# An encoder kernel on one core: the first sum of a layer's seven-product units, put behind the last combination of the right sides

## The chip, the cores and the metric

The kernel runs on one core of a Trainium2 chip. The metric is the device time in microseconds (us) of one execution; smaller is better. The engines of the core work side by side, each through its own queue of instructions in order: TensorE (PE: matmuls, and PEld: its weight loads), VectorE (DVE), ScalarE (ACT), GpSimd (POOL) and SyncE (SP). In this kernel SP issues nearly all loads, and POOL issues the accumulating loads. Matmuls read SBUF and write PSUM, which has eight banks; the kernel uses them as four pairs, named acc, sc, o and aux.

## The reference

Two layers of a bidirectional encoder over a sequence of 512 rows of width 1024, in float32. Each layer has a mixing part (retention heads and differential attention heads behind one input projection, and an output projection) and then a gated feed-forward part, which is the one that matters here:

```
h = rms_norm(x, ffn_norm_g[l])
x = x + (silu(h @ w_gate[l]) * (h @ w_up[l])) @ w_down[l]
```

`w_gate` and `w_up` are 1024 x 2816, `w_down` is 2816 x 1024. The normalisation scales each row of x by one over its root mean square and each column by `ffn_norm_g`.

## The kernel before

The activations are kept transposed: `x` is eight tiles of 128 features by 512 rows. Every product is done to full precision by splitting both sides into a high part (a cast on ACT) and a low part (the remainder, a subtraction on DVE) and adding three matmuls: high by high, high by low, low by high (`mm3`, lines 204 to 208). So each weight that arrives by DMA first costs one ACT cast (line 194) and one DVE subtraction (line 198), and each activation likewise (lines 223 and 224, in `split`).

The feed-forward part takes the 22 blocks of 128 columns of the gate and up projections in four groups, `FFN = [(0, 4), (4, 12), (12, 18), (18, 22)]`. After each group comes the down projection of that group, `for m in range(KT)` (lines 818 to 847): for each of eight column blocks m of the output, the weights of the group are loaded (two column blocks at a time in the first group), split (lines 194 and 198), multiplied into a PSUM bank, and added to `x[m]` by a DVE addition, `residual`, line 634. The banks come in turn from acc, sc and o, two of each, so six column blocks can be under way; blocks 6 and 7 need banks that the residuals of blocks 0 and 1 have emptied.

The first group is done plainly (`gate_up`, lines 681 to 695). The other three use units of seven products in place of eight for a pair of 2 x 2 blocks (`seven`, lines 751 to 797). For that the right sides, that is the halves of the normalised `x`, must be added and subtracted with one another once in each layer. This is `combine(i)` (lines 715 to 736), called four times: `combine(0)` to `combine(2)` while the plain group runs, after its blocks 1, 2 and 3 (line 805), and `combine(3)` inside the first down projection, after its column block 1 (line 845). Each makes, on DVE, the scaled halves `b1`, `b2` (line 719), four sums `ta` and `tb` (lines 721 to 724), and the splits of all of them (lines 712, 728 and, through `split`, 224). The split of `tb` (line 730) comes last.

The left sides are combined too, for each unit. A unit has two rows of weights of 128 x 1024 in `in_wgu`. It loads one block twice into a tile by a broadcast load (line 756, SP), loads another block (line 757, SP) and the second row (line 758, SP), and has two more blocks added to the first tile on their way in, by an accumulating load (line 759, POOL):

```
nc.gpsimd.dma_start(sums, src[:, 0::3], accum_op=ALU.add)
i = nc.vector.tensor_tensor(a[:, T:], a[:, :T], s31[:, T:], op=ALU.add)
```

Line 760 is the sum that this case is about: it reads what the accumulating load has left, and line 763 adds its result to the second row's first half (`s4`). Then come the unit's casts and splits (lines 740 and 741, in `split_in`, and `split` for `s4`) and its 84 matmuls of 128 x 256 (line 775). The tile of a (and of the sum) is called s or raw in the profile, in turn from unit to unit; in the first unit of a layer the sum is s<-s,raw.

The order of the work on each engine is not written in the kernel: the Tile framework puts it out by its own model of times and priorities, from the order of the code and the dependencies. The kernel can add an ordering edge, `tc.add_manual_dep(later, earlier, order, ...)`, which says that one instruction is put behind another; between instructions of one engine it costs no semaphore. Before the change the sum of each unit has such an edge to the last split of the unit before, kept in `last_split[0]` (lines 741, 761 and 762). The first unit of a layer has none, since `last_split[0]` is `None` there.

Of the kernel before, what the change touches and what calls it, by code (L numbers as in the profile page):

```python
# [11 lines left out]
ALU = mybir.AluOpType  # L12
# [42 lines left out]
def encoder_kernel(ctx: ExitStack, tc: tile.TileContext, xT, wfirst, wsingle, wvv, wout, wgu, wdn, prm, lam, cst, outT):  # L55
    nc = tc.nc
# [14 lines left out]
    def big(s, dt=F32, tag="w", bufs=NW):  # L71
        return tpool.tile([P, T], dt, tag=tag, name=nm(s), bufs=bufs)
# [19 lines left out]
    def f32(ap):  # L92
        return ap.bitcast(F32)
# [42 lines left out]
    def column_sums(ps, w, src):  # L136

        hi, lo = split(src, "w", NW)
        nc.tensor.matmul(ps, w, hi, start=True, stop=False)
        sums[0] = nc.tensor.matmul(ps, w, lo, start=False, stop=True).ins.name  # L140
# [40 lines left out]
    def pair():  # L181

        t = tpool.tile([P, 2, T], F32R, tag="h", name=nm("h"), bufs=8)
        return t[:, 0], t[:, 1]
# [25 lines left out]
    def cut(pair, *idx):  # L210
        return tuple(t[idx] for t in pair)
# [9 lines left out]
    def split(src, tag, bufs):  # L221
        hi, lo = pair() if tag == "h" else [big(n, F32R, tag, bufs) for n in ("hi", "lo")]
        nc.scalar.copy(hi, src)
        nc.vector.tensor_tensor(lo, src, f32(hi), op=ALU.subtract)
        return hi, lo

    def rsqrt(out, src, scale):

        func(out, src, AF.Ln, bias=eps_sb, scale=scale)
        func(out, out, AF.Exp, scale=-0.5)  # L230
# [79 lines left out]
    def layer(l, n1, h, x_src, first_raw):  # L310
# [76 lines left out]
        def diff_head(hd, qs, ks, v):  # L387
# [42 lines left out]
            rsqrt(sq, ss, 1.0 / P)  # L430
            nc.vector.scalar_tensor_tensor(sq, o, gd[:, l : l + 1], sq, op0=ALU.mult, op1=ALU.mult)
            mix[4 + hd] = split(sq, "mix", NMIX)
            yield

        def ret_pair(pr):
# [80 lines left out]
            nc.vector.scalar_tensor_tensor(sq, o, prm_sb[:, PRM_RG + l : PRM_RG + l + 1], sq, op0=ALU.mult, op1=ALU.mult)  # L516
            nc.vector.tensor_tensor(sq, sq, gates[pr], op=ALU.mult)
            mix[pr] = split(sq, "mix", NMIX)
            yield "norm"

# [182 lines left out]


        H1, H2 = slice(0, C), slice(C, T)
        comb = []

        def part256(src):
            hi = tpool.tile([P, 256], F32R, tag="dv", name=nm("bh"), bufs=16)
            lo = tpool.tile([P, 256], F32R, tag="dv", name=nm("bl"), bufs=16)  # L710
            nc.scalar.copy(hi, src)
            nc.vector.tensor_tensor(lo, src, f32(hi), op=ALU.subtract)
            return hi, lo

        def combine(i):

            b1, b2 = big("b"), big("b")
            for t, kt in ((b1, i), (b2, i + 4)):
                nc.vector.scalar_tensor_tensor(t, x[kt], prm_sb[:, PRM_FG + 8 * l + kt : PRM_FG + 8 * l + kt + 1], rstd2, op0=ALU.mult, op1=ALU.mult)
            ta, tb = big("ta"), big("tb")  # L720
            nc.vector.tensor_tensor(ta[:, H1], b1[:, H1], b1[:, H2], op=ALU.subtract)
            nc.vector.scalar_tensor_tensor(ta[:, H2], ta[:, H1], -1.0, b2[:, H2], op0=ALU.mult, op1=ALU.subtract)
            nc.vector.tensor_tensor(tb[:, H1], b2[:, H2], b1[:, H2], op=ALU.subtract)
            nc.vector.scalar_tensor_tensor(tb[:, H2], ta[:, H2], -1.0, b2[:, H1], op0=ALU.mult, op1=ALU.subtract)
            b11, b21 = part256(b1[:, H1]), part256(b2[:, H1])
            b22 = big("b22", F32R, *[("w", NW), ("qk", NQK), ("mix", NMIX), ("mix", NMIX)][i])
            nc.scalar.copy(b22[:, H1], b2[:, H2])
            nc.vector.tensor_tensor(b22[:, H2], b2[:, H2], f32(b22[:, H1]), op=ALU.subtract)
            ta = split(ta, "mix", NMIX)
            tb = split(tb, *(("mix", NMIX) if i else ("qk", NQK)))  # L730
            comb.append(
                dict(
                    b11=b11, b21=b21, b22=(b22[:, H1], b22[:, H2]),
                    t1=cut(ta, slice(None), H1), t2=cut(ta, slice(None), H2), t3=cut(tb, slice(None), H1), t4=cut(tb, slice(None), H2),
                )
            )
# [9 lines left out]
            fours[0] += 1  # L746
            return new_chunk(1024)[0] if fours[0] % 2 else tpool.tile([P, 1024], F32, tag="ah", name=nm("s"), bufs=NAH)

        fours, last_split = [0], [None]

        def seven(ff, act, tag, bufs):

# [46 lines left out]
        for a0, a1 in FFN:  # L799
            act, last = [], a1 == FT  # L800
            if a1 <= PLAIN:
                for ff in range(a0, a1):
                    act.append(gate_up(ff, *(("mix", NMIX) if ff < 2 else ("rn", 4))))
                    if ff:
                        combine(ff - 1)
            else:
                units = []
                for ff in range(a0, a1):
                    tag = ("h", 8) if not last else ("mix", NMIX) if ff < a0 + 2 else ("rn", 4)
                    units.append(seven(ff, act, *tag))  # L810
                next(units[0])
                for i, unit in enumerate(units):
                    next(unit)
                    if i + 1 < len(units):
                        next(units[i + 1])
                    next(unit, None)
            n = (a1 - a0) * P
            for m in range(KT):

                both = 2 * n <= 1024  # L820
                if not both or m % 2 == 0:
                    new = new_chunk(n * (1 + both), 1)
                    for i in range(1 + both):
                        nc.sync.dma_start(new[0][:, i * n : (i + 1) * n], wdn[l, m + i][:, a0 * P : a1 * P])
                    ww = split_chunk(*new)
                w = cut(ww, slice(None), slice(m % 2 * n, (m % 2 + 1) * n)) if both else ww
                if last and l + 1 == DEPTH and m == KT - 1:

                    for t, queue in ((H1, nc.sync), (H2, nc.scalar)):
                        ps = any_bank()  # L830
                        for i, a in enumerate(act):
                            mm3(ps[:, :C], cut(w, slice(None), slice(i * P, (i + 1) * P)), cut(a, slice(None), t), i == 0, i == a1 - a0 - 1)
                        nc.vector.tensor_tensor(x[m][:, t], x[m][:, t], ps[:, :C], op=ALU.add)
                        queue.dma_start(outT[m][:, t], x[m][:, t])
                    continue
                ps = any_bank()
                for i, a in enumerate(act):
                    mm3(ps, cut(w, slice(None), slice(i * P, (i + 1) * P)), a, i == 0, i == a1 - a0 - 1)
                if last and l + 1 < DEPTH:
                    residual(m, x[m], ps, n3, h3, PRM_AG + 8 * (l + 1))  # L840
                    nc.sync.dma_start(xscr[m], x[m])
                else:
                    residual(m, x[m], ps, None, None, None)
                    if a1 <= PLAIN and m == 1:
                        combine(PLAIN - 1)
                    if last:
                        nc.sync.dma_start(outT[m], x[m])
# [10 lines left out]
    for l in range(DEPTH):  # L858
        if l:
            raws = [load_chunk(wfirst[l, c]) for c in range(4)]  # L860
        n, h = layer(l, n, h, xT if l == 0 else xscr, raws)
# [89 lines left out]
```

## Time and profile before

| what | us |
|---|---|
| median of 3 runs | 1265.05 |
| lowest and highest run | 1262.17 and 1267.66 |
| the profiled execution | 1264.07 |
| its span, from first to last instruction | 1262.3 |
| TensorE busy | 1247.4 |
| DVE busy | 915.8 |
| ACT busy | 674.1 |

The first down projection of layer 0 begins at about 324 us of the span, the first seven-product unit at about 350 us; in layer 1 these are about 948 and 976 us. A row of a view in order of time has the start, the duration, the engine, the line of the kernel, the operation, the tile written and the tiles read (buffer numbers left out), the shapes, the count, and in brackets the idle time of the engine ahead of it with the party that ended it. The duration of a matmul is longer than the distance to the next one's start, because matmuls overlap; so distances between starts count for TensorE. The granted clock is the share of TensorE's full clock.

### The profile page before, as it was taken

To read this page: it belongs to the slowest core of one execution; us is meant where nothing else is said; L and a number is where in the kernel's file an instruction comes from. 1 tells how busy PE (TensorE), PEld (TensorE's weight loads), DVE (VectorE), ACT (ScalarE), POOL (GpSimd) and SP (SyncE) were. 2 spreads that over 40 slices of the span, in tenths; PEclk is the share of its full clock that TensorE was granted. 3 is DMA by queue.
4 is the path that set the end of the run, shared out by engine and by line. 5 is a ranking of instruction groups with operands and counts; after the bars stand their busy time and mean duration, and the time that the engine had idled before them with its cause. 6 is when DMAs were issued, how large, how long until landed. Compare 5 with 4: busy or idle time off the path is not lost.

```text
span 1262.3 us, 19138 instructions
## 1 busy us (share of the span) xinstructions
PE 1247.4 (99%) x7516; PEld 1100.3 (87%) x7516; DVE 915.8 (73%) x1514; ACT 674.1 (53%) x1106; POOL 61.4 (5%) x78
## 2 busy tenths in 40 slices
PE   9999999999899999999999999999999999999998
PEld 7878988778799989989888889987887999899897
DVE  6899768867877546747568997697778775576574
ACT  6778746555445425525448785565553553254251
POOL 1000000000011001000000000000000110000000
PEclk9999999999999999999999999999999999999999
DMA  7222223243277537646342122142333774476452
GB/s 264 84 68 67 68 67 125 68 116 101 71 176 174 166 102 166 163 114 151 110 156 84 51 84 67 51 150 77 99 101 84 174 182 129 119 180 152 122 140 84
DMA packets 58842, 148.48 MB, mean 118 GB/s; under 512 B 5632, under 2 KB 5888, under 8 KB 58624
## 3 DMA queue, kind: packets, MB, share of 16 engines
q1 hardware_dynamic: 48528, 127.95, 32.8%
q0 software_dynamic: 9792, 18.88, 9.4%
q8 instruction: 59, 0.97, 0.3%
q10 hardware_dynamic: 432, 0.44, 0.1%
q14 instruction: 31, 0.25, 0.1%
HBM read 143.05 MB, written 4.19 MB: 117 GB/s over the span
## 4 chain that ended last, share of the span: by engine, by line
PE 94%; DVE 3%; DMA 1%; ACT 1%; issue 0%; ACTq 0%
PE acc L775 16%; PE acc L205 11%; PE acc L207 11%; PE acc L206 11%; PE o L775 8%; PE o L205 4%; PE o L207 4%; PE sc L775 4%; PE o L206 4%; PE sc L207 4%; PE sc L205 4%; PE sc L206 3%; PE sc L400 2%; PE o L501 2%; PE sc L485 1%; DMA raw<-in_wgu 1%
## 5 line engine op out<-in xcount | busy, mean ns | idle before, releaser
L194 ACT CAST hi<-raw 128x1024 fp32r<-128x1024 f32 (+2 forms) x139 | 138.2, 1002 | 185.8 <-issue 49.2
L198 DVE TENSOR_TENSOR lo<-raw,hi 128x1024 fp32r<-128x1024 f32 (+2 forms) x140 | 162.1, 1162 | 58.8 <-ACT hi L194 58.4
L205 PE MATMUL acc<-h,hi 128*128 128x512 f32 x406 | 160.1, 396 | 0.6 <-ACT hi L194 0.6
L206 PE MATMUL acc<-h,hi 128*128 128x512 f32 x406 | 159.4, 393 | 0.0
L207 PE MATMUL acc<-h,lo 128*128 128x512 f32 x406 | 159.4, 393 | 0.0
L775 PE MATMUL acc<-hi,hi 128*128 128x256 f32 x432 | 123.2, 285 | 0.0
L775 PE MATMUL acc<-hi,lo 128*128 128x256 f32 x432 | 122.3, 283 | 0.0
L775 PE MATMUL acc<-lo,hi 128*128 128x256 f32 x432 | 122.3, 283 | 0.0
L740 ACT CAST hi<-raw 128x1024 fp32r<-128x1024 f32 x54 | 56.7, 1050 | 72.3 <-PE acc L775 42.2
L741 DVE TENSOR_TENSOR lo<-raw,hi 128x1024 fp32r<-128x1024 f32 x54 | 66.2, 1225 | 38.1 <-ACT hi L740 38.1
L740 ACT CAST hi<-s 128x1024 fp32r<-128x1024 f32 x54 | 56.6, 1048 | 67.3 <-issue 25.6
L205 PEld LDWEIGHTS acc<-h,hi 128*128 128x128 f32 x406 | 76.5, 189 | 17.6 <-ACT hi L194 1.9
L207 PEld LDWEIGHTS acc<-h,lo 128*128 128x128 f32 x406 | 76.6, 189 | 16.1 <-DVE lo L198 0.2
L206 PEld LDWEIGHTS acc<-h,hi 128*128 128x128 f32 x406 | 76.6, 189 | 15.2
L741 DVE TENSOR_TENSOR lo<-s,hi 128x1024 fp32r<-128x1024 f32 x54 | 66.2, 1226 | 25.4 <-ACT hi L740 25.4
L775 PEld LDWEIGHTS acc<-lo,hi 128*128 128x128 f32 x432 | 82.9, 192 | 0.2
L775 PEld LDWEIGHTS acc<-hi,hi 128*128 128x128 f32 x432 | 82.7, 192 | 0.2
L775 PEld LDWEIGHTS acc<-hi,lo 128*128 128x128 f32 x432 | 82.8, 192 | 0.0
L106 ACT ACTIVATE g<-g 128x512 f32<-128x512 f32 x44 | 27.8, 632 | 52.7 <-DVE g L793 47.8
L106 ACT ACTIVATE sc<-sc,mx 128x512 f32<-128x512 f32 x64 | 46.0, 720 | 18.4 <-DVE mx L404 17.9
L205 PE MATMUL sc<-h,hi 128*128 128x512 f32 x142 | 55.5, 394 | 0.0
L206 PE MATMUL sc<-h,hi 128*128 128x512 f32 x142 | 55.4, 390 | 0.0
(235 smaller groups left out, 3500.4 us busy)
## 6 DMA issues: line engine op xcount, KB each, us to landing
raw<-in_wgu SPq DMA_DIRECT2D x52, 512.0 KB, 4.2
s<-in_wgu SPq DMA_DIRECT2D x36, 512.0 KB, 4.7
raw<-in_wsingle SPq DMA_DIRECT2D x32, 512.0 KB, 3.6
s<-in_wgu POOLq DMA_DIRECT2D x18, 512.0 KB, 6.4
raw<-in_wgu POOLq DMA_DIRECT2D x18, 512.0 KB, 7.3
raw<-in_wvv SPq DMA_DIRECT2D x16, 512.0 KB, 3.6
raw<-in_wout SPq DMA_DIRECT2D x16, 512.0 KB, 3.6
raw<-in_wdn SPq DMA_DIRECT2D x32, 256.0 KB, 2.9
```

What stands on the lines that cost most here:

```text
L106: i = nc.scalar.activation(out, src, f, **kw).ins
L194: c = nc.scalar.copy(hi[:, s], raw[:, s])
L198: nc.vector.tensor_tensor(lo[:, s], raw[:, s], f32(hi[:, s]), op=ALU.subtract)
L205: first = nc.tensor.matmul(out, L[0], R[0], start=start, stop=False)
L206: nc.tensor.matmul(out, L[0], R[1], start=False, stop=False)
L207: nc.tensor.matmul(out, L[1], R[0], start=False, stop=stop)
L400: nc.tensor.matmul(ps, q[m][:, t], k[m][part], start=part == 0, stop=part == 1)
L485: nc.tensor.matmul(out, ks[hh][part][:, sb], qs[hh][:, tb], start=part == 0, stop=part == 1)
L501: i = nc.tensor.matmul(o[b, c * C : (c + 1) * C], v[pr // 2][2 * c + j][:, (pr % 2) * P + hh * HD : (pr % 2) * P + (hh + 1) * HD], s[c][:, ...
L740: nc.scalar.copy(hi, raw)
L741: last_split[0] = nc.vector.tensor_tensor(lo, raw, f32(hi), op=ALU.subtract).ins.name
L775: nc.tensor.matmul(ps[:, :C], L[x1], R[x2], start=start and k + i == 0, stop=k == 3 and i == 2, skip_group_check=True)
```

## The change

`split` keeps the name of its last subtraction. `combine` copies it into `last_split[0]` after the split of `tb`, and `last_split` is made ahead of `combine`. `combine(3)` is the last of a layer's four, and the units come after it in the code, so the first unit of each layer now finds a name there, and its sum of line 760 gets the ordering edge that the other units' sums have. The sums of the later units have the edges they had.

```
     def split(src, tag, bufs):
         hi, lo = pair() if tag == "h" else [big(n, F32R, tag, bufs) for n in ("hi", "lo")]
         nc.scalar.copy(hi, src)
-        nc.vector.tensor_tensor(lo, src, f32(hi), op=ALU.subtract)
+        splits[0] = nc.vector.tensor_tensor(lo, src, f32(hi), op=ALU.subtract).ins.name
         return hi, lo
+
+    splits = [None]
...
-        comb = []
+        comb, last_split = [], [None]
...
             ta = split(ta, "mix", NMIX)
             tb = split(tb, *(("mix", NMIX) if i else ("qk", NQK)))
+            last_split[0] = splits[0]
...
-        fours, last_split = [0], [None]
+        fours = [0]
```

## The prediction

> **What bounds the kernel now.** I read the page first: the busy times and the chain that ended last, by engine.
>
> ```profile
> PE 1247.4 (99%) x7516; PEld 1100.3 (87%) x7516; DVE 915.8 (73%) x1514; ACT 674.1 (53%) x1106; POOL 61.4 (5%) x78
> ...
> PE 94%; DVE 3%; DMA 1%; ACT 1%; issue 0%; ACTq 0%
> ```
>
> TensorE is the bound, and only its waits and slow stretches can be won. The few per cent of DVE and DMA on the chain are the place to look. Next: the sum of line 760, on VectorE (DVE), by its instances in time. Here are the first of layer 0, one of a later block, and the first of layer 1.
>
> ```profile
> 335.30 0.69 DVE L760 TENSOR_TENSOR s<-s,raw 128x512 f32<-128x512 f32 x1 [4.04 <-DMA raw<-in_wgu]
> ...
> 464.82 0.69 DVE L760 TENSOR_TENSOR s<-s,raw 128x512 f32<-128x512 f32 x1 [8.94 <-DMA raw<-in_wgu]
> ...
> 959.48 0.69 DVE L760 TENSOR_TENSOR s<-s,raw 128x512 f32<-128x512 f32 x1 [3.63 <-DMA raw<-in_wgu]
> ```
>
> The two sums that the change touches hold DVE for 4.04 and 3.63 us until the accumulating load lands. A DVE stall need not cost anything: at 464.82 one of 8.94 us does not. So I looked at TensorE in three stretches, then at its rows in the two that suffer. The columns of the first view are: stretch, its length, then busy time with count for PE, weight loads, DVE, ACT, POOL; then granted clock, DMA share and GB/s.
>
> ```profile
> 330.00:350.00 20.00, 16.77 (x72) 12.86 (x72) 15.96 (x29) 6.83 (x11) 0.00 (x0) 1.00 0.22 49
> 455.00:466.00 11.00, 11.00 (x50) 9.13 (x49) 2.06 (x3) 1.05 (x1) 1.20 (x1) 1.00 0.50 112
> 955.00:976.00 21.00, 17.86 (x71) 13.67 (x70) 16.46 (x30) 6.56 (x11) 0.00 (x0) 0.92 0.28 65
> ```
> ```profile
> 339.57 0.39 PE L206 MATMUL o<-lo,hi 128*128 128x512 f32 x1
> 339.79 0.39 PE L207 MATMUL o<-hi,lo 128*128 128x512 f32 x1
> 342.16 0.47 PE L205 MATMUL acc<-hi,hi 128*128 128x512 f32 x1 [1.98 <-DVE x L634]
> ...
> 343.27 0.50 PE L205 MATMUL sc<-hi,hi 128*128 128x512 f32 x1 [0.41 <-DVE x L634]
> ...
> 345.61 0.50 PE L207 MATMUL acc<-hi,lo 128*128 128x512 f32 x1 [0.63 <-DVE lo L198]
> ...
> 350.31 0.28 PE L775 MATMUL acc<-bh,lo 128*128 128x256 f32 x1
> 350.43 0.28 PE L775 MATMUL acc<-bh,hi 128*128 128x256 f32 x1
> ...
> 964.39 0.39 PE L207 MATMUL acc<-hi,lo 128*128 128x512 f32 x1
> 966.34 0.47 PE L205 MATMUL sc<-hi,hi 128*128 128x512 f32 x1 [1.56 <-DVE x L634]
> ...
> 969.78 0.80 PE L207 MATMUL sc<-hi,lo 128*128 128x512 f32 x1 [1.17 <-DVE lo L198]
> 970.38 0.63 PE L205 MATMUL sc<-hi,hi 128*128 128x512 f32 x1
> 970.80 0.63 PE L206 MATMUL sc<-lo,hi 128*128 128x512 f32 x1
> ...
> 976.16 0.28 PE L775 MATMUL acc<-bh,lo 128*128 128x256 f32 x1
> ```
>
> At 455 to 466 TensorE is busy 11.00 of 11.00 us under the longest stall; in the other two stretches it loses over 3 us each. There the released party is named: first the residuals of line 634, which empty the six banks of the down projection, then the weight split of line 198. Both stand in DVE's queue behind the stalled sum. The chain of waits from 320 to 372 us tells it in one piece:
>
> ```profile
> 327.44 7.83 DMA raw<-in_wgu
> ...
> 338.27 0.60 DVE s L763
> ...
> 341.42 0.60 DVE x L634
> ...
> 344.41 1.15 DVE lo L198
> ```
>
> **The size of the hole.** A long matmul (128x512) starts 0.227 us after the last (339.57 to 339.79 and the rows' rounding), a short one (128x256) 0.12 us (350.31 to 350.43). Between 339.79 and 350.31 stand the 24 long matmuls of the last two column blocks, 6 and 7, and 4 short ones of the first unit. Without waits, the next short one would start at 339.79 + 0.23 + 24 x 0.227 + 4 x 0.12 = 345.94; it starts at 350.31. Layer 0 loses **4.37 us**. In layer 1 the same 28 would end at 964.39 + 0.23 + 5.92 = 970.54, and the next starts at 976.16: **5.62 us**, of which 1.5 us are not waits but slow matmuls (the pitch from 970.38 to 970.80 is 0.42 us in place of 0.23, and the granted clock of this stretch is 0.92 where layer 0 has 1.00). At most **10.0 us** can be won.
>
> The Trainium skill, "TensorE: Matmul & The Clock Gate", section "What's actually happening", says that the clock falls to half after an idle window of about 3.4 us. No single gap here is above 2 us, and layer 0 with the longer gap keeps 1.00, so by that rule the slow spell need not belong to the stall and would stay; the sum below would then be 1.5 us smaller. The trace has the spell right behind the gaps of this place, so I let it go with them.
>
> **What the change does to DVE's queue.** It adds no instruction, no byte and no semaphore: it puts an ordering edge from the first sum of a layer to the last split of the last combination (lines 224 and 730). Both are on DVE. What it moves is the sum (335.30) and, since that needs its result, the sum of line 763; their cast of line 740 on ACT and split of line 741 follow. No DMA moves ahead with them: the accumulating load goes out at 327.44 whatever DVE does, and lands 7.83 us later, at 335.27. These rows carry the working, DVE in layer 0:
>
> ```profile
> 341.33 0.69 DVE L634 TENSOR_TENSOR x<-x,acc 128x512 f32<-128x512 f32 x1
> ...
> 344.32 1.23 DVE L198 TENSOR_TENSOR lo<-raw,hi 128x1024 fp32r<-128x1024 f32 x1
> ...
> 346.05 0.70 DVE L224 TENSOR_TENSOR lo<-tb,hi 128x512 fp32r<-128x512 f32 x1
> ```
> ```profile
> 337.53 0.39 PE L207 MATMUL acc<-hi,lo 128*128 128x512 f32 x1
> ...
> 962.12 0.39 PE L207 MATMUL sc<-hi,lo 128*128 128x512 f32 x1
> ```
>
> I replay the queue in its present order, with the two sums taken out and put behind the row at 346.05.
>
> 1. The stall goes: DVE goes on at 331.26 in place of 335.30, and at 955.85 in place of 959.48.
> 2. From the sum to the first residual DVE spends 341.33 - 335.30 = 6.03 us, of which the sums are 0.61 and 0.60. So it reaches the first residual 4.82 us after it goes on, at 336.08 (layer 1: 960.67).
> 3. That residual now waits for TensorE instead: column block 0 ends at 337.53 + 0.39 = 337.92 (962.51), the residual starts 0.04 later, at 337.96 (962.55). So 1.88 us of the gain turn into a new wait. This is what is late next.
> 4. From there to the end of the weight split DVE takes 344.32 + 1.23 - 341.33 = 4.22 us: 342.18 (966.77). The first matmul that needs it can start 0.06 later (345.55 to 345.61), at 342.24 (966.83).
> 5. TensorE would want it at 340.02 + 4 x 0.227 + 4 x 0.12 = 341.41 (in layer 1 only two short ones stand ahead: 964.62 + 0.91 + 0.24 = 965.77). A wait of 0.83 (1.06) us stays. The residuals of blocks 0 and 1 are done by 339.8, before their banks are wanted at 340.02, so the waits of 1.98, 1.56 and 0.41 us go.
> 6. The moved sum: the last split comes 346.05 - 341.33 = 4.72 us after the first residual, at 342.68; the sum then stands at 343.28 and ends at 343.97, 8 us after the data landed. Its cast takes 1.04 us and its split 1.23 us, so the low half is there at about 346.4. TensorE comes to it at 345.94 + 0.83 = 346.77. It is covered by block 7's matmuls, with 0.4 us to spare. If that cover is gone, each us by which the sum is later costs one us of TensorE.
>
> Sum: layer 0 gains 4.37 - 0.83 = 3.54, layer 1 gains 5.62 - 1.06 = 4.56, together **8.1 us**. The profiled execution took 1264.07 us (span 1262.3 and 1.8 around it), which makes **1256.0 us**. The median of the runs is 1 us above the profiled one, and the runs spread over 1262.17 to 1267.66, so the same gain may read as 1257.
>
> The unknown is the order that the framework writes for DVE, ACT and TensorE once the edge is there. Its bounds: if the two splits of the last combination (0.60 each) are put into the wait of step 3, and nothing else, the weight split ends up to 1.2 us earlier, the waits of step 5 go almost wholly, and the gain is up to 10.0 (1254.1). If the two sums are put ahead of the weight split, it ends 1.2 us later in each layer: gain 5.7 (1258.4). I take the order as it is, in the middle.
>
> **Rivals.**
>
> *The edge changes nothing* (the sum still stands where it stalls, or the last split is written ahead of 335.27): 1264. For it: DVE could reach the last split by 336.7 if the order were free. Against: that is already after the landing. Chance 0.05.
>
> *The sums go ahead of the weight split of blocks 6 and 7*, as bounded above: 1258.4. For it: DVE has 1.88 us to fill while it waits for block 0. Against: the splits stand in that room as well. Chance 0.18.
>
> *The sum slips behind the last residual* (block 7), since the residuals stand earlier in the code than the units: then it starts only after block 7's last matmul, about 346.93 + 0.04 + 0.60 = 347.57, its cast ends at 349.35, its split at 350.6. TensorE comes to the low half at 350.6 instead of 350.31 in layer 0, and at 970.54 + 1.06 + 3.83 = 975.4 instead of 976.16 in layer 1. About no change, 1263.7. Against: today splits of the first unit stand between the residuals of blocks 5, 6 and 7. Chance 0.10.
>
> *Slower: the sum slips behind the split of the unit's second load.* That split waits for a buffer that block 7's weights leave:
>
> ```profile
> 350.29 1.05 ACT L740 CAST hi<-raw 128x1024 fp32r<-128x1024 f32 x1 [5.60 <-PE sc L206]
> ```
>
> In the new time that cast starts at about 346.7, the split runs from 347.8 to 349.0, then come sum, cast and split: 352.0. TensorE waits 5.2 us, 1.7 more than today in layer 0 and 0.7 in layer 1, and after a gap that long I take the slow spell of 1.5 us in both: 1264.07 + 5.4 = 1269.5. It decides from the point where the sum starts later than 350.31 - (0.69 + 1.04 + 1.23 + 0.10) = 347.25. Against: the code has the sum ahead of that split, and the sum would be ready 12 us earlier. Chance 0.07.
>
> **How the numbers follow.** The forecast (1254.1 to 1257.5) has 0.60. Range 1253 to 1261: with the forecast and the second rival it holds 0.78 of the chance; the lower end is the full 10.0 us and one for the spread of the runs, the upper a gain of 3. A measurement of this kernel tells about 0.5% from no change, which is 6.3 us: faster means under 1258.7. The forecast lies under it but for 0.02, the second rival on it, by half. Faster 0.58 + 0.09 = 0.67; same 0.02 + 0.09 + 0.05 + 0.10 = 0.26; slower 0.07.
>
> **What would show it.** Step 1: the first sum of each layer without idle time put down to the DMA. Step 3: an idle time of 1 to 2 us at the first residual of line 634, released by TensorE. Step 5: one TensorE wait of about 1 us on the split of line 198 in each layer, none on line 634. Step 6: no TensorE wait on lines 740 or 741. The clock: 1.00 in layer 1's stretch; if the slow spell stays without a gap ahead of it, I was wrong on it. If a wait on the first unit's low half takes the hole's place, or the sum comes after block 7's residual, the forecast is wrong; so it is if TensorE's hole closes and the time does not fall, which would say that later units are bound by something else.

## The result, and the profile after

The changed kernel takes 1255.59 us (median of 5 runs, 1255.13 to 1257.47) against 1265.38 for the kernel before (5 runs, 1262.17 to 1267.66). The ratio is 0.9925, with a 95% interval of 0.9907 to 0.9944: faster by 0.75%, or about 9.5 us, and 0.4 us from the time forecast. In a second comparison, on another occasion, the same two kernels stand at 0.9932 (0.9916 to 0.9947). The profiled execution of the changed kernel took 1255.13 us, with a span of 1253.4.

The page of the changed kernel, busy times and the chain by engine:

```profile
PE 1242.5 (99%) x7516; PEld 1097.1 (88%) x7516; DVE 915.4 (73%) x1514; ACT 675.1 (54%) x1106; POOL 61.4 (5%) x78
...
PE 97%; DVE 2%; ACT 1%; DMA 0%; issue 0%; ACTq 0%
```

TensorE's share of the chain goes from 94 to 97%, that of DVE from 3 to 2%, that of the DMA from 1% to nothing. The work is the same: the count of each engine has not moved. (Outside these counts the prediction's "no semaphore" is off by two: ACT has 287 semaphore instructions in place of 285.) VectorE (DVE) in order of time, layer 0, changed kernel (its lines are numbered two to three higher: 636 is the residual, 744 and 763 are the split and the sum, 766 the sum of `s4`):

```profile
333.87 0.68 DVE L224 TENSOR_TENSOR lo<-ta,hi 128x512 fp32r<-128x512 f32 x1
335.81 0.69 DVE L636 TENSOR_TENSOR x<-x,acc 128x512 f32<-128x512 f32 x1 [1.27 <-PE acc L207]
336.42 0.69 DVE L224 TENSOR_TENSOR lo<-tb,hi 128x512 fp32r<-128x512 f32 x1
337.02 0.69 DVE L763 TENSOR_TENSOR s<-s,raw 128x512 f32<-128x512 f32 x1
...
339.42 1.22 DVE L198 TENSOR_TENSOR lo<-raw,hi 128x1024 fp32r<-128x1024 f32 x1
...
341.15 0.69 DVE L766 TENSOR_TENSOR s<-raw,s 128x512 f32<-128x512 f32 x1
```

The sum has no idle time ahead of it. It stands right behind the last split of the last combination (336.42), as the edge asks. Of the waits for the accumulating load, six with 32.4 us together before, the four of later blocks are left. From the waits of DVE (engine, line, party waited for, us in total, times, longest):

```profile
DVE s L763 <- DMA raw<-in_wgu: 25.7, 4, 8.6
```

DVE's own idle time in the place is now at the first residual, 1.27 us, and it is TensorE that ends it. TensorE in the same kernel, the start of the first down projection, its waits, and the first low half of the first unit, in layer 0 and then in layer 1:

```profile
321.56 0.39 PE L205 MATMUL acc<-hi,hi 128*128 128x512 f32 x1
...
337.66 0.39 PE L207 MATMUL o<-hi,lo 128*128 128x512 f32 x1
...
339.65 0.36 PE L778 MATMUL acc<-bh,hi 128*128 128x256 f32 x1 [0.56 <-DVE x L636]
...
340.69 0.50 PE L207 MATMUL acc<-hi,lo 128*128 128x512 f32 x1 [0.32 <-DVE lo L198]
...
345.36 0.28 PE L778 MATMUL acc<-bh,lo 128*128 128x256 f32 x1
...
943.11 0.39 PE L205 MATMUL sc<-hi,hi 128*128 128x512 f32 x1
...
962.24 0.50 PE L207 MATMUL sc<-hi,lo 128*128 128x512 f32 x1 [1.17 <-DVE lo L198]
...
967.13 0.28 PE L778 MATMUL acc<-bh,lo 128*128 128x256 f32 x1
```

The waits of 1.98 and 1.56 us on the residuals are gone; what is left in both layers ends with the weight split of line 198. In what follows the place is measured by one number, its **length**: from the start of block 5's last matmul to the start of the first unit's first low half. 24 long and 4 short matmuls lie between, which make 6.15 us without waits (0.23 + 24 x 0.227 + 4 x 0.12). The view of stretches gives length, busy times and granted clock in one row. Before, and then changed:

```profile
339.79:350.31 10.52, 7.29 (x30) 5.01 (x29) 10.52 (x18) 4.91 (x9) 0.00 (x0) 1.00 0.12 40
964.39:976.16 11.77, 8.63 (x30) 6.07 (x29) 10.72 (x17) 4.73 (x7) 0.00 (x0) 0.86 0.22 67
```
```profile
337.66:345.36 7.70, 6.82 (x30) 5.08 (x29) 7.70 (x12) 2.62 (x3) 0.00 (x0) 1.00 0.16 53
959.20:967.13 7.93, 6.76 (x30) 5.06 (x29) 7.93 (x12) 2.83 (x4) 0.00 (x0) 1.00 0.18 59
```

The spans differ by 8.9 us. By the marks in the profiles, 2.82 us of it lie in layer 0's place and 3.84 us in layer 1's. Another 2.1 us lie ahead of both and have nothing to do with the change: the first down projection starts at 321.56 here, and before at

```profile
323.70 0.39 PE L205 MATMUL acc<-hi,hi 128*128 128x512 f32 x1
...
948.30 0.39 PE L205 MATMUL sc<-hi,hi 128*128 128x512 f32 x1
```

Between the two places 0.24 us are won (597.99 us from 350.31 to 948.30, 597.75 from 345.36 to 943.11), and behind the second 0.1 us are lost.

### The profile page after: what moved, and what is told of

Read it like the earlier page. It is cut to its first block, busy times and chain, and to the rows that moved or that the text cites. A ratio compares the mean times of both kernels' runs of the same rounds, so it can differ in the third digit from the quotient of the medians.

```text
span 1253.4 us, 19140 instructions
## 1 busy us (share of the span) xinstructions
PE 1242.5 (99%) x7516; PEld 1097.1 (88%) x7516; DVE 915.4 (73%) x1514; ACT 675.1 (54%) x1106; POOL 61.4 (5%) x78
## 4 chain that ended last, share of the span: by engine, by line
PE 97%; DVE 2%; ACT 1%; DMA 0%; issue 0%; ACTq 0%
PE acc L778 17%; PE acc L205 11%; PE acc L207 11%; PE acc L206 11%; PE o L778 8%; PE o L205 4%; PE o L207 4%; PE o L206 4%; PE sc L778 4%; PE sc L207 4%; PE sc L205 4%; PE sc L206 4%; PE sc L402 2%; PE o L503 2%; PE sc L487 1%; PE aux L418 1%
## 5 line engine op out<-in xcount | busy, mean ns | idle before, releaser
L206 PE MATMUL sc<-h,hi 128*128 128x512 f32 x142 | 55.3, 389 | 0.0
L207 PE MATMUL sc<-h,lo 128*128 128x512 f32 x142 | 55.3, 389 | 0.0
```

The lines of the kernel that those rows point to most:

```text
L206: nc.tensor.matmul(out, L[0], R[1], start=False, stop=False)
L207: nc.tensor.matmul(out, L[1], R[0], start=False, stop=stop)
```

## The experiments

**Both kernels once more.** Theory and rival on the half-clock spell and the start are in the expectations.

> The kernel before, unchanged, profiled a second time. Between the two profiles on record 2.1 us of the difference lie in the first 10 us of the span, where TensorE leaves its half clock at about 10.4 us before and 6.5 us after, and 1.5 us are the half-clock spell in layer 1's place. Theory: both belong to the clock's own timing and not to the edge; then this profile shows the stalls of about 4.0 and 3.6 us again and a length from block 5's last matmul to the first unit's low half of 10.2 to 10.8 us in layer 0 and 10.2 to 11.8 in layer 1, while the start may lie anywhere between 6.5 and 10.4. Rival: the slow spell belongs to the hole; then it comes back in layer 1, or comes in layer 0, and a length without it is not seen. Ratio 1.000 within 0.002.

> The changed kernel, unchanged, profiled a second time. Theory (the half-clock spells of 3.4 us belong to the holes and not to a place): lengths of 7.7 and 7.9 us again, granted clock 1.00 in both places, and what differs in the span from the first profile lies in the first 10 us. Rival (spells come at random): a spell in one of the two places. Ratio to the kernel before 0.991 to 0.994.

The kernel before took 1263.68 us against itself at 1265.53 (0.9987, 0.9976 to 0.9998), which shows what such a comparison can tell: less than 0.25% is not to be read. Its two places, and those of the changed kernel's second profile:

```profile
338.45:349.53 11.08, 8.49 (x31) 5.91 (x29) 11.05 (x18) 5.04 (x9) 0.00 (x0) 0.85 0.14 47
963.61:976.14 12.53, 9.76 (x31) 7.03 (x29) 10.85 (x18) 4.94 (x8) 0.00 (x0) 0.73 0.26 70
```
```profile
338.02:345.73 7.71, 6.84 (x30) 5.09 (x29) 7.71 (x12) 2.62 (x3) 0.00 (x0) 1.00 0.15 51
960.32:968.26 7.94, 6.77 (x31) 5.08 (x30) 7.94 (x12) 2.83 (x4) 0.00 (x0) 1.00 0.18 60
```

The lengths of the changed kernel repeat to 0.01 us, with the clock at 1.00. The span of its second profile is 1.0 us longer, and of that only 0.37 us lie ahead of the first down projection (321.93 against 321.56); 0.74 us lie between the two places (598.49 us from 345.73 to 944.22), so the theory that the difference lies in the first 10 us fell for the larger part. Those of the kernel before do not: the slow spell came in layer 0 this time too (0.85) and was longer in layer 1 (0.73), so my theory for that profile, that the spell belongs to the clock's own timing, fell, and so did its bounds (11.08 and 12.53 against at most 10.8 and 11.8). The rival held: the spell belongs to the hole. (The expectation's 6.5 us for the changed kernel's start is a misreading: the clock records of its trace are at full from 4.3 us on, and those of the kernel before from 10.4 us on.) The start, on the other hand, does vary by itself: this time the down projection began at 322.35 in the kernel before and at 321.93 in the changed one. Over two profiles of each, the places give 10.80 - 7.71 = 3.1 and 12.15 - 7.94 = 4.2 us, together 7.3.

**One layer at a time.**

```
-            last_split[0] = splits[0]
+            last_split[0] = splits[0] if l == 0 else None
```

> The change with the edge in layer 0 alone. Theory (each layer's sum costs TensorE on its own): layer 0's length 7.7 us as after, layer 1's 10.2 to 11.8 as before; time 1259 to 1262. Rival (the gain is one effect of the whole schedule): both lengths as before or both as after, time near 1265 or 1256.

1260.34 us, ratio 0.9961 (0.9948 to 0.9975). Its stretches, and its sum in layer 1:

```profile
337.66:345.36 7.70, 6.82 (x30) 5.09 (x29) 7.70 (x12) 2.62 (x3) 0.00 (x0) 1.00 0.16 53
959.21:971.28 12.07, 8.78 (x31) 6.19 (x30) 10.88 (x18) 4.87 (x8) 0.00 (x0) 0.86 0.22 68
```
```profile
954.45 0.69 DVE L763 TENSOR_TENSOR s<-s,raw 128x512 f32<-128x512 f32 x1 [3.77 <-DMA raw<-in_wgu]
```

Layer 0 is as in the changed kernel; layer 1 is as before, with the stall, the long hole and the slow clock. Its 12.07 us are above the 11.8 expected, but within the 11.77 to 12.53 of the kernel before. So each layer's sum costs TensorE on its own.

**The wait without the place.** The sum stays where it was, but in the first unit of a layer it does not read what the accumulating load leaves, so this kernel leaves that part of the sum out:

```
-            i = nc.vector.tensor_tensor(a[:, T:], a[:, :T], s31[:, T:], op=ALU.add)
+            first = last_split[0] is None
+            i = nc.vector.tensor_tensor(a[:, T:], a[:, :T], a[:, :T] if first else s31[:, T:], op=ALU.add)
+            if first:
+                tc.add_manual_dep(i.ins, old_place[0], order, reason="old place")
```

`old_place[0]` is the subtraction of line 728 in `combine(2)`, behind which the sum stands in the kernel before; DVE's order around the place is the same.

> The kernel before with the sum held at its old place, but in the first unit of a layer it adds the first block to itself and does not read what the accumulating load leaves (so it leaves that addition out); no other wait, no order is moved. Theory (the wait for the load is the whole cost, its place none): no stall at the sum, and since the two sums run in time that DVE spends waiting for block 0, the weight split ends earlier than in the changed kernel: length 6.9 to 7.3 us in both layers against 7.7 and 7.9 after, time 1254 to 1256. Rival (what helps is that the combination's work is put ahead of the sum): length 9 us or more, time 1262 to 1266.

1255.60 us, ratio 0.9922 (0.9907 to 0.9938).

```profile
329.48 0.69 DVE L763 TENSOR_TENSOR s<-s 128x512 f32<-128x512 f32 x1
...
336.26 0.69 DVE L634 TENSOR_TENSOR x<-x,acc 128x512 f32<-128x512 f32 x1 [0.67 <-PE acc L207]
...
339.26 1.22 DVE L198 TENSOR_TENSOR lo<-raw,hi 128x1024 fp32r<-128x1024 f32 x1
```
```profile
338.11:345.20 7.09, 6.44 (x30) 5.10 (x29) 7.09 (x11) 2.44 (x5) 0.00 (x0) 1.00 0.18 58
959.31:966.65 7.34, 6.44 (x30) 5.16 (x29) 7.34 (x11) 2.68 (x5) 0.00 (x0) 1.00 0.20 64
```

With the old order and no wait, the whole gain is there, and the places are 0.6 us shorter than in the changed kernel, as expected: the sum of line 760 then runs ahead of block 0's residual, in time that DVE would wait anyway (its idle time there is 0.67 in place of 1.27). So the wait for the load was the whole of what the change wins; of the holes, 7.09 - 6.15 = 0.94 and 7.34 - 6.15 = 1.19 us are left without it. The order that the edge brings costs one sum, 0.6 us, in each layer.

**Too far behind.** The edge goes to the last residual of the first down projection:

```
+            last_res[0] = nc.vector.tensor_tensor(xt, xt, ps, op=ALU.add).ins.name
...
                     if a1 <= PLAIN and m == 1:
                         combine(PLAIN - 1)
+                    if a1 <= PLAIN and m == KT - 1:
+                        last_split[0] = last_res[0]
```

> The change with the edge moved: the first sum stands behind the last residual of the first down projection. Theory (the sum is covered by block 7's matmuls and no further; from there each us later costs one): block 7 ends, then residual 0.6, sum 0.7, cast 1.05, split 1.2 us before the low half is there: length 10 to 11 us in each layer, time 1261 to 1265, the gain gone though no stall on the load is left. Rival (TensorE has enough other work of the unit): length under 8.5 us, time 1255 to 1257.

1267.75 us, ratio 1.0018 (1.0009 to 1.0028): the gain is gone, and no time is won back; by the comparison of the kernel before with itself, whether it is slower than before is not to be told. DVE, TensorE and the stretches:

```profile
347.22 0.69 DVE L638 TENSOR_TENSOR x<-x,sc 128x512 f32<-128x512 f32 x1 [1.58 <-PE sc L207]
347.82 0.68 DVE L765 TENSOR_TENSOR s<-s,raw 128x512 f32<-128x512 f32 x1
```
```profile
349.71 0.39 PE L780 MATMUL acc<-bh,hi 128*128 128x256 f32 x1 [2.53 <-ACT hi L745]
...
350.66 0.38 PE L780 MATMUL o<-hi,hi 128*128 128x256 f32 x1 [0.45 <-ACT hi L745]
```
```profile
339.93:351.00 11.07, 6.95 (x30) 5.05 (x29) 7.56 (x12) 2.38 (x3) 0.00 (x0) 1.00 0.07 24
967.73:978.82 11.09, 6.96 (x31) 5.06 (x29) 7.56 (x12) 2.39 (x3) 0.00 (x0) 1.00 0.08 25
351.00:362.00 11.00, 10.06 (x71) 9.79 (x69) 5.71 (x8) 3.91 (x7) 1.21 (x1) 0.84 0.53 137
```

The stall on the load is gone here too, DVE even idles, and TensorE waits as long as before, now for the cast of line 745, which comes behind the sum. The theory's mechanism held; its upper ends (11 us, 1265) were a little low. What it left out comes behind the place: in layer 0 the slow spell (0.84 from 351 to 362), and in both layers a later wait in the first unit, 0.94 and 1.06 us, again for line 745.

**The wait that is left.** Three kernels move DVE's order around the weight split of blocks 6 and 7 (`wsplit[0]`); the diff is that of the second, in which `held` keeps the residuals of blocks 2 and 3 back. The first has no `held`, and the third sets `last_split[0]` between the splits of `ta` and `tb` instead. The first puts the sum behind it; the second puts the residuals of blocks 2 and 3 behind it too; the third ties the sum to the split of `ta` in place of that of `tb`, into DVE's idle time, and holds the two residuals as the second does.

```
                     ww = split_chunk(*new)
+                    if a1 <= PLAIN and m == 6:
+                        last_split[0] = wsplit[0].name
+                        for j, pj in held:
+                            residual(j, x[j], pj, None, None, None, last_split[0])
...
+                elif a1 <= PLAIN and m in (2, 3):
+                    held.append((m, ps))
```

> The change with the edge moved: the first sum stands behind the weight split of column blocks 6 and 7 in place of the combination's last split. Theory (the length left over is DVE's chain from block 0's residual to that weight split, and the sum ahead of it costs its own 0.6 us): length 7.1 and 7.3 us, 1.2 us off the changed kernel's time, 1254 to 1255. Rival (the weight split is set by its cast or by the load): length 7.7 and 7.9 as after.

> As the one before, and the residuals of column blocks 2 and 3 stand behind the weight split too, since their banks are wanted later. Theory: the split ends 1.8 us earlier than in the changed kernel, and then the cast of these weights or the first unit's low half is last; length 6.2 to 6.9 us in both layers, 2 to 3 us off the changed kernel's time, 1252.5 to 1254. Rival (another party takes over at once): length over 7.2.

> The edge goes to the split of the last combination's ta, one split earlier, so that the sum falls into DVE's wait of 1.3 us for block 0, and the residuals of blocks 2 and 3 stand behind the weight split. Theory (the data landed before that place and DVE waits there anyway): no idle time at the sum put down to the load, the sum costs nothing; only line 766's sum stays ahead of the weight split, which ends 1.2 us earlier than after; length 6.4 to 6.8 us, 1252.5 to 1254. Rival (the load lands too late for that place): an idle time of up to 1.5 us at the sum, length 7.5 or more.

One stretch of each, layer 0 (layer 1 is within 0.01 us):

```profile
338.01:345.58 7.57, 6.43 (x30) 5.08 (x29) 7.57 (x12) 2.97 (x4) 0.00 (x0) 1.00 0.15 52
```
```profile
338.36:344.93 6.57, 6.54 (x31) 5.04 (x29) 6.57 (x11) 3.16 (x4) 0.00 (x0) 1.00 0.11 40
```
```profile
337.59:344.57 6.98, 6.43 (x31) 5.09 (x29) 6.98 (x11) 2.45 (x4) 0.00 (x0) 1.00 0.17 57
```

The first is shorter by 0.13 us in layer 0 and 0.36 in layer 1, not by 0.6. Its weight split does end 0.6 us earlier, counted from the start of the down projection (340.39 - 321.92 = 18.47 against 340.64 - 321.56 = 19.08), but the short matmuls that stood in the wait in the changed kernel (four in layer 0, two in layer 1, 0.12 us each) now stand behind block 7, and the wait is bare:

```profile
340.44 0.50 PE L209 MATMUL acc<-hi,lo 128*128 128x512 f32 x1 [1.14 <-DVE lo L200]
```

The second comes within 0.42 us of 6.15, and the third takes the sum into DVE's idle time with no wait for the load, as its theory says:

```profile
334.39 0.69 DVE L767 TENSOR_TENSOR s<-s,raw 128x512 f32<-128x512 f32 x1
335.75 0.69 DVE L638 TENSOR_TENSOR x<-x,acc 128x512 f32<-128x512 f32 x1 [0.67 <-PE acc L209]
```

The third's length, 6.98, is above the 6.4 to 6.8 expected, for the same reason as the first's: its weight split ends 1.2 us earlier than in the changed kernel (338.16 + 1.22 - 321.50 = 17.88), as the theory has it, and the four short matmuls behind block 7 give 0.48 of that back. In time, none of the three is told from the changed kernel: 1255.07 (0.9927, 0.9912 to 0.9941), 1255.59 (0.9925, 0.9910 to 0.9941) and 1255.49 (0.9925, 0.9909 to 0.9940) beside 1255.85 (0.9932, 0.9916 to 0.9947) for the changed kernel in the same comparison. The first had been expected at 1254 to 1255, the other two at 1252.5 to 1254, and these two forecasts failed, though the second's length is the expected one. For the second its profile says where it went: from the first place to the second down projection it takes 601.62 us, and the changed kernel 597.75. The accumulating load, DVE and TensorE, a little later:

```profile
352.06 1.20 POOL L766 DMA_DIRECT2D raw<-in_wgu  x1 [25.12 <-DMA raw<-in_wgu]
```
```profile
360.34 0.69 DVE L767 TENSOR_TENSOR s<-s,raw 128x512 f32<-128x512 f32 x1 [2.74 <-DMA raw<-in_wgu]
```
```profile
363.80 0.38 PE L782 MATMUL acc<-bh,hi 128*128 128x256 f32 x1 [1.53 <-DVE u L802]
```

Now it is the third unit's sum that waits for its accumulating load, and TensorE waits behind it; the same comes once more at 582 us. That load stands behind the broadcast load into the same tile and goes out at 352.06, 29.79 us after the start of the down projection, where the changed kernel has 349.95 - 321.56 = 28.39; why is not shown. Such loads took between 5.7 and 8.5 us to land in the changed kernel. For the third kernel no such wait stands in its one profile. That profile's span of 1251.6 us is shorter than the changed kernel's 1253.4 by about what its two places save (0.72 and 0.94 us), but it was taken in the fastest of the kernel's six runs (1253.38), and four of them took 1255.46 or more. Why those are not shorter stays open.

## Why the prediction was right

*The hole and its cause* were read rightly: the rows named the residuals and the weight split, and the run without the wait shows that the load stands behind all of it but 0.94 and 1.19 us.

*Steps 1 to 3* came as written. The load did not move: it went out 327.44 - 323.70 = 3.74 us after the start of the down projection before, and 325.15 - 321.56 = 3.59 us after it now. ("Whatever DVE does" says too much: POOL waits for a weight split on DVE ahead of it, but one that the change does not touch.) The stalls went, and the first residual now waits for block 0. The wait is 1.27 us and not 1.88, since the split of `ta` was put into it, as one bound of the order had it.

*Step 4* failed by one term. The weight split ends 19.08 us after the start of the down projection, where the replay had 342.18 - 323.70 = 18.48. I had left the order as it was and both sums behind the weight split; one of the two, the first unit's sum itself (337.02), was put ahead of it. That is half of the rival in which both go ahead, and it costs what a sum costs, 0.6 us. (The split of `tb` went ahead with it and that of `ta` into the wait of step 3; these two cancel.) In the run without the wait, which keeps the order that the replay assumed, the split ends at 339.26 + 1.22 - 322.01 = 18.47: the replay itself was right, and the order was not.

*Step 5* therefore came out at 7.70 - 6.15 = 1.55 and 7.93 - 6.15 = 1.78 us of loss in place of 0.83 and 1.06; with the assumed order, in the run without the wait, it is 0.94 and 1.19. I had said that no wait on the residuals would be left; 0.56 us of layer 0's loss is put down to one, for the bank of the first unit's first product, and not for blocks 6 and 7.

*Step 6* had the sum 19.6 us after the start of the down projection (343.28 - 323.70). It is 4 us earlier, at 15.46, because the split of `tb` was put right behind the first residual on DVE (336.42), with its cast ahead of the weight cast on ACT (333.64 against 336.09). So its cover is ample and not 0.4 us. The price given for a lost cover was tried in the kernel with the edge behind the last residual: the sum starts at 347.82 there, 347.68 on the clock of the profile before, later than the 347.25 from which I had it decide, and the place is 11.07 us long against 10.52. The rival priced at no change came out at 1.0018.

*The sum* was 3.54 + 4.56 = 8.1 us. The two places of the first pair of profiles give 2.82 + 3.84 = 6.7; over two profiles of each kernel they give 7.3, because the kernel before loses more to the slow clock than its first profile shows, 1.5 us in one layer. The runs say 8.6 and 9.5, each within about 2 us. The rest, 1 to 2 us, is not settled; it is of the size by which the start of the span varies. So it is in part luck that the forecast's 1256.0 lies 0.4 us from the measured time: the order cost 1.4 us more than forecast, the hole had been dearer than the one profile showed, and the unsettled rest made up for what was missing.

*The clock.* I had let the slow spell go with the hole, and it did. Of the 13 places of 8 us or less in these profiles none has a granted clock under 1.00; of the 7 of 10.5 us or more, five have the spell, in the place or right behind it. The rule of the Trainium skill that the prediction set against it ("TensorE: Matmul & The Clock Gate", section "What's actually happening": half clock after an idle window of about 3.4 us) would have left the spell in place, if it is read as one unbroken gap; the traces do not bear that reading out.

## What to carry to other kernels

A stall on an in-order engine costs what stands behind it in the queue: the two stalls of 4.04 and 3.63 us cost TensorE 7.9 us together (10.52 - 7.09 and 11.77 - 7.34, against the run without the wait), one of 8.94 us in the same kernel nothing; so read its price on the bounding engine, over the stretch where it lies. Where the data cannot come earlier, put the instruction that waits behind work that does not need it, but not past the point where its own followers are wanted: counted from the start of the down projection, the data here landed at 11.6 us (335.27 - 323.70), the sum did well at 12.9 (334.39 - 321.50) and at 15.5, and at 24.0 (347.82 - 323.84) it cost the whole gain. And count what an ordering edge puts ahead of the next bound: one moved sum, 0.6 us, was more than a third of the 1.55 us left to win in that place.

## What was not expected of the hardware

TensorE's half-clock spells come after holes made of several gaps, none above 2.1 us in the kernel before, while TensorE was still busy 7 to 10 of the 11 to 12.5 us. A spell of 3.4 us costs up to about 1.5 us, by matmuls that start every 0.42 us (970.38 to 970.80) in place of 0.227, and less where waits fall into it: layer 0's place is 11.08 us long with a spell and 10.52 without. So a hole can be dearer in one execution than in another, and the kernel without holes is also the steadier one (its first five runs lie within 2.3 us, those of the kernel before within 5.5; the last two kernels above, with shorter places still, spread over 3.9 and 3.6). The first 10 us of a span vary too: in ten profiles of code that is the same up to there, the first down projection starts between 321.5 and 323.8 us. In the clock records of the traces TensorE is at its full clock from 4.3 to 10.6 us on, and the two profiles in which that comes last (10.4 and 10.6) are those with the latest starts (323.70 and 323.84).
